# Putting the short contractions of two token mixers on all 128 rows of TensorE

## The chip, the cores and the metric

The kernel runs on one core of a Trainium2 chip. The metric is the device time of one execution in microseconds (us), and lower is better. A core has a matrix engine (TensorE, PE in the profile, with its weight loads listed apart as PEld), a vector engine (VectorE, DVE), a scalar engine (ScalarE, ACT), GpSimd (POOL) and SyncE (SP, here a DMA queue). A matmul contracts over the partitions (rows) of its two operands: the stationary one is loaded first, then the moving one streams past it. The profile writes the stationary operand as rows*columns and the moving one as rows x columns, so `16*128 16x256` is a contraction over 16 rows.

## The reference

A hybrid encoder of two layers works on 528 tokens (16 learned meta tokens and 512 others) with 1024 features. Each layer is a SwiGLU feed-forward half (hidden size 2816), a mixer, and a second feed-forward half. The change is in the mixer alone, which is cut here to what it touches:

```python
h = z @ w_in                       # one wide projection, split into the operands below
# branch A: gated linear attention, 4 heads, 64 key and 128 value features, forward and backward
gate = log_sigmoid(lr @ w2 + b2) / 16          # lr: 16 features for each direction (low rank)
b = cumsum(gate) inside a chunk
att = mask((q * exp(b)) @ (k * exp(-b)).T)     # scores inside a chunk, both directions
o_a = att @ v + (q * exp(b)) @ S               # S: state carried over the chunks
# branch B: softmax attention, 8 query heads on 2 key/value heads, 64 features each
p = softmax(rope(norm(q)) @ rope(norm(k)).T)
o_b = p @ v                                    # 528 keys: 4 blocks of 128 and 16 meta keys
y = sigmoid(g_a) * (o_a @ w_pa) + sigmoid(g_b) * (o_b @ w_pb)
out = y @ w_out
```

The last layer needs no output at the meta tokens, so most of its tensors are 512 wide, not 528.

## The kernel before

All activations are kept with features on partitions and tokens on the free axis. A product with a weight matrix runs in a split form: weight and operand each become a rounded part (`hi`, written by ACT) and a remainder (`lo`, written by DVE), both in the rounded matmul format fp32r, and three of the four partial products are accumulated. In the projections of the mixer that is three matmuls for each of eight 128-row slices and each half of the tokens (264 wide), 48 in all. In the narrow low-rank projection (32 columns) it is 48 as well. Weights come in slabs of 1024 columns over SP's queue, and `Weights.make` splits each of them up to four slabs ahead of its use.

Plain fp32 matmuls stand in the profile with two records each, fp32r matmuls and transposes with one.

The mixer (`mixer`) does in turn:

- four products for `r` and the low-rank product (into `lr`, 32 rows and a row of ones for the bias);
- twice (`gla_pair`, two heads each): projections of q, k and v; for each direction the decays, `z = w2t.T @ lr` on 33 rows; transposes of k and v to tokens on partitions; the end states of the blocks (`state(b)`, forward in rows 0 to 63 and backward in rows 64 to 127); the scores (64 rows: a head each in rows 0 to 63 and 64 to 127, two directions `d`) and the output, which adds `vtok @ scores` and `state(b) @ qin`. In the last block, NB - 1, only the forward state exists, so its product runs on 64 rows; for the meta block only the backward one does;
- `attention`: for two key/value heads, pairs of 128-query blocks. `probs` makes one block's scores and their softmax, `weighted` transposes the probabilities, splits them and multiplies by v. The 16 meta keys are a fifth part, the tail: a transpose to 16 partitions, a copy by ACT (`hi`), a subtraction by DVE (`lo`), and two matmuls on 16 rows. `weighted` runs 18 times in the first layer and 16 times in the second, so there are 34 tails;
- gates, merging, and the last product.

A scheduler orders the instructions of each engine, from the order in the code, the dependencies and its own costs. PE thus has projections of later steps (`project`, tiles `mm`) between the steps of the linear attention and of the softmax attention. Each engine then runs its list in that order.

Of the kernel before, what the change touches and what calls it, by code (L numbers as in the profile page):

```python
# [141 lines left out]
class Weights:  # L142
# [91 lines left out]
    def next(self, name):  # L234
        t = PLAN[self.pos]
        assert t[1] == name, (t, name)
        s, c = divmod(COLUMN[self.pos], SLAB)
        self.pos += 1
        hi, lo = self.use(self.at[s])
        return hi[:, c : c + t[5]], lo[:, c : c + t[5]]  # L240

    def op(self, *load):

# [5 lines left out]
def build(tc, ctx, xt, wts, win, par, w2, const, umask, out):  # L249
# [32 lines left out]
    def nm(p):  # L282
        count[0] += 1
        return f"{p}{count[0]}"
# [300 lines left out]
    def gla_pair(l, p, lr, w2t, sr, qa, ka, va, n_out):  # L585
# [17 lines left out]
        for d in range(2):  # L603
            z = pair()
            for i, hs in enumerate(halves):
                c0 = p * 256 + d * P
                TE.matmul(z[:, i, :HF], w2t[:33, c0 : c0 + P], lr[:33, hs], start=True, stop=True)
            a, g, c, ct_ = slot("t"), slot("t"), slot("t"), slot("t")

            S.activation(v2(a), z[:, :, :HF], AF.Abs)  # L610
            S.activation(a, a, AF.Exp, scale=-1.0)
            S.activation(a, a, AF.Ln, bias=1.0)
            V.scalar_tensor_tensor(v2(g), z[:, :, :HF], 0.0, v2(a), ALU.min, ALU.subtract)
            ones = ct[:, C_COS + SEQ : C_COS + SEQ + 1]
            for bs in [b[1] for b in blocks] + [MB]:
                n = bs.stop - bs.start
                V.tensor_tensor_scan(c[:, bs], ones.broadcast_to([P, n]), g[:, bs], 0.0, ALU.mult, ALU.add)
            mid = blk(c)[:, :, 63:64].broadcast_to([P, NB, P])
            tot = blk(c)[:, :, 127:128].broadcast_to([P, NB, P])
            mm_ = c[:, T - 1 : T].broadcast_to([P, META])  # L620
            r16 = 1.0 / 16.0
            src = c
            if d == 1:
                V.tensor_tensor(g, c, g, ALU.subtract)
                src = g

            def to_end():
                V.tensor_tensor(blk(ct_), blk(src), tot, ALU.subtract)
                V.tensor_tensor(ct_[:, MB], src[:, MB], mm_, ALU.subtract)


# [24 lines left out]
            if d == 0:  # L656
                S.activation(c, c, AF.Exp, scale=r16)
                ein, eq, ek = c, a, g
            else:
                S.activation(ct_, ct_, AF.Exp, scale=-r16)  # L660
                ein, eq, ek = ct_, g, a
            V.tensor_tensor(qp[:, :n_out], qa, eq[:, :n_out], ALU.mult)
            V.tensor_tensor(kp, ka, ek, ALU.mult)
            if qin is None:
                qin = [slot("p"), slot("p")]
            e0 = 127 if d == 0 else 0
            for hh in range(2):
                rows = slice(hh * HD, (hh + 1) * HD)
                to = slice(d * HD, (d + 1) * HD)
                V.tensor_tensor(qin[hh][to, :n_out], qa[rows], ein[rows, :n_out], ALU.mult)  # L670
                V.tensor_copy(dec[to, hh, :], blk(ein)[rows, :, e0])
            prods.append((qp, kp))
# [14 lines left out]
        def vtok(b, hh):  # L687
            return ktm[:META, 256 + hh * P : 256 + (hh + 1) * P] if b == NB else vk[hh][:, blocks[b][1]]

        for b in [NB, 0, 1, 2, 3]:  # L690
            ps = sm()
            for hh in range(2):
                TE.matmul(ps[:, hh * P : (hh + 1) * P], ktok(b, hh), vtok(b, hh), start=True, stop=True)  # L693
            pv = ps[:, :256].rearrange("p (h v) -> p h v", h=2)
            nxt = 0 if b == NB else b + 1
            if b == NB:
                S.copy(state(0)[0:HD], pv[0:HD])
            elif b < NB - 1:
                for hh in range(2):
                    V.scalar_tensor_tensor(state(nxt)[0:HD, hh], state(b)[0:HD, hh], dec[0:HD, hh, b : b + 1],  # L700
                                           pv[0:HD, hh], ALU.mult, ALU.add)
            if b != NB:
                prv = NB if b == 0 else b - 1
                S.copy(state(prv)[HD:P], pv[HD:P])
# [7 lines left out]
        for b in [3, 2, 1, 0] + [NB] * (n_out == T):  # L712
# [1 line left out]
            tt = slot("t")  # L714
            t3 = tt[:n, : 2 * n].rearrange("p (h i) -> p h i", h=2)
            ats = pair()
            for hh in range(2):
                rows = slice(hh * HD, (hh + 1) * HD)
                for d in range(2):
                    TE.matmul(ats[:n, hh, d * n : (d + 1) * n], prods[d][1][rows, bs], prods[d][0][rows, bs],  # L720
                              start=True, stop=True)

# [2 lines left out]
            op = sm()  # L725
            for hh in range(2):
                os_ = op[:, hh * n : (hh + 1) * n]
                rows = slice(0, P) if b < NB - 1 else (slice(0, HD) if b == NB - 1 else slice(HD, P))
                TE.matmul(os_, vtok(b, hh), t3[:, hh], start=True, stop=False)  # L729
                TE.matmul(os_, state(b)[rows, hh], qin[hh][rows, bs], start=False, stop=True)  # L730
            for hh in range(2):
# [22 lines left out]
    def attention(l, x, rs, n_out):  # L754
# [11 lines left out]
        vp, vpm = vpp[:, 0], vpp[:, 1]  # L766
        for c in range(NB):
            TE.transpose(vp[:, c * P : (c + 1) * P], vt[:, c * P : (c + 1) * P], ident)
        TE.transpose(vpm[:META, :P], vt[:, MB], ident)
        vs = []  # L770
        for g in range(2):
            rows = slice(g * HD, (g + 1) * HD)
            vv = slot("k", F32R)
            vm = small.tile([META, P], F32R, tag="vm", name=nm("vm"), bufs=2)
            v3 = vv[:, :512].rearrange("p (c f) -> p c f", c=NB)
            src = vp.rearrange("p (c f) -> p c f", c=NB)[:, :, rows]
            S.copy(v3[:, :, 0:HD], src)
            V.tensor_tensor(v3[:, :, HD:P], src, v3[:, :, 0:HD].bitcast(F32), ALU.subtract)
            S.copy(vm[:, 0:HD], vpm[:META, rows])
            V.tensor_tensor(vm[:, HD:P], vpm[:META, rows], vm[:, 0:HD].bitcast(F32), ALU.subtract)  # L780
            vs.append((v3, vm))

        bt = [None] * 4
# [47 lines left out]
        def group(g, ctx):  # L831
# [23 lines left out]
            def weighted(prs, n):  # L855
# [14 lines left out]
                o = sm()  # L870
                tp = o[:, 256:512]
                for u, pr in enumerate(prs):
                    TE.transpose(tp[:META, u * n : (u + 1) * n], pr[:n, MB], ident[:n, :n])
                tail = slot("lr", F32R)
                hi, lo = tail[:META, :256], tail[:META, 256:512]
                S.copy(hi[:, :w], tp[:META, :w])
                V.tensor_tensor(lo[:, :w], tp[:META, :w], hi[:, :w].bitcast(F32), ALU.subtract)
                parts.append((vs[g][1], hi[:, :w], lo[:, :w]))
                for i, (vw, ph, pl) in enumerate(parts):
                    TE.matmul(o[:, :w], vw, ph, start=i == 0, stop=False)  # L880
                    TE.matmul(o[:, :w], vw, pl, start=False, stop=i == len(parts) - 1)  # L881
                return o

            def both_rows(j, cs, o):
# [33 lines left out]
    def mixer(l, norm, done, following):  # L918
# [1 line left out]
        x, n_out = norm.x, T if l < DEPTH - 1 else SEQ  # L920
        pools = open_pools("left", e=8, i=5, p=7, q=6, k=5, lr=1)
        banks = open_pools("left", psum=("mm", "sm"), mm=2, sm=2)
        w2t = one.tile([33, 512], F32, tag="w2", name=nm("w2"))
        S.dma_start(w2t, w2[l])
        rp = [product("w_in", Acc(k, n_out), x, KC) for k in ("ss", "sm", "mm")]
        rs = norm.rs()
# [5 lines left out]
            sr.append(r)  # L932
        table("natural_log_exp_and_others")
        lr = slot("lr")
        ps = product("w_in", Acc("sm"), x, KC, width=32)
        scaled(lr, ps, rs, 1.0, slice(0, 32))
        V.memset(lr[32:33], 1.0)
        for p in range(2):
            qa = project(x, rs, "i", 0.125, n_out)
            ka = project(x, rs, "i")  # L940
# [153 lines left out]
```

## Time and profile before

| | |
|---|---|
| median of 3 runs | 2274.95 us (2274.92 to 2277.56) |
| the profiled execution: its own time | 2273.0 us |
| its span, first to last instruction | 2271.2 us |
| granted TensorE clock, mean | 0.992 |
| first mixer, about | 350 to 860 us of the span |
| second mixer, about | 1490 to 1960 us |

The profiled execution is 1.95 us below the median. Busy times of PE are modelled and overlap, since matmuls are pipelined: what a matmul costs in a full stream is the step from its start to the start of the next one, not its duration. In a timeline, consecutive instructions of one form are merged into one row, with the start of the first and their number.

### The profile page before, as it was taken

The page shows a single profiled execution, that of the slowest core. Times are in us where ns is not written, and L with a number is a line of the kernel's source. Part 1 is how long each engine was busy: PE and PEld are TensorE (multiplying, and loading weights), DVE is VectorE, ACT ScalarE, POOL GpSimd, SP SyncE. Part 2 cuts the span into 40 slices and gives each one's busy share as a digit, 9 for nine tenths or more (in the row PEclk, how much of TensorE's full clock was granted, in tenths as well). Part 3 has the DMA queues.
Part 4 walks back from the last instruction along what each step waited for, and adds up shares of the span by engine and source line. Part 5 has one row for each costly group of instructions (what it writes and reads, how often), then busy time and mean ns, then how long its engine had stood idle before and what let it go on. Part 6 is the DMA issues. An engine that isn't in the chain of part 4 may idle for free.

```text
span 2271.2 us, 39827 instructions
## 1 busy us (share of the span) xinstructions
PE 2219.0 (98%) x16548; PEld 2105.0 (93%) x16548; DVE 1512.6 (67%) x2387; ACT 1192.1 (52%) x1761; POOL 159.3 (7%) x186
## 2 busy tenths in 40 slices
PE   6999999999999999999989999999999999999997
PEld 5999999989999999999989999998788888989896
DVE  6657567476876676565676565674868667756566
ACT  7535355354785574453565353543457846636353
POOL 1111010000000010101001110100000001101010
PEclk9999999999999999999989999999999999999998
DMA  8868572212113485867657685632121136858661
GB/s 229 236 157 225 142 174 94 75 49 75 38 38 112 121 215 151 198 171 175 178 145 197 153 219 148 167 102 75 57 67 46 47 121 169 211 157 216 166 174 59
DMA packets 88412, 315.19 MB, mean 139 GB/s; under 512 B 9830, under 2 KB 12262, under 8 KB 88232
## 3 DMA queue, kind: packets, MB, share of 16 engines
q1 hardware_dynamic: 61136, 218.26, 28.9%
q0 software_dynamic: 25344, 92.29, 22.9%
q8 instruction: 130, 2.13, 0.4%
q10 hardware_dynamic: 1752, 2.11, 0.3%
q14 instruction: 50, 0.41, 0.1%
HBM read 264.38 MB, written 2.10 MB: 117 GB/s over the span
## 4 chain that ended last, share of the span: by engine, by line
PE 94%; DVE 3%; ACT 1%; DMA 1%; issue 0%; SPq 0%; DVEq 0%; POOL 0%; ACTq 0%
PE ss L497 39%; PE ss L377 27%; PE mm L377 15%; PE sm L377 3%; PE sm L863 1%; PE sm L880 1%; PE ss L838 1%; PE sm L881 1%; PE ss L383 1%; PE ss L839 1%; PE sm L693 1%; PE ss L720 0%; PE sm L729 0%; DVE wlo L222 0%; PE sm L730 0%
## 5 line engine op out<-in xcount | busy, mean ns | idle before, releaser
L497 PE MATMUL ss<-xc,whi 128*128 128x264 f32 (+1 forms) x4928 | 901.4, 285 | 25.4 <-ACT whi L221 9.2
L497 PEld LDWEIGHTS ss<-xc,whi 128*128 128x128 f32 x4928 | 766.2, 189 | 28.0 <-ACT whi L221 9.9
L497 PE MATMUL ss<-xc,wlo 128*128 128x264 f32 (+1 forms) x2464 | 701.7, 285 | 3.5 <-DVE wlo L222 3.5
L377 PE MATMUL ss<-g,whi 128*128 128x264 f32 (+2 forms) x2668 | 494.2, 301 | 0.0
L497 PEld LDWEIGHTS ss<-xc,wlo 128*128 128x128 f32 x2464 | 465.6, 189 | 4.5 <-DVE wlo L222 4.3
L377 PEld LDWEIGHTS ss<-g,whi 128*128 128x128 f32 x2668 | 388.6, 188 | 17.4
L377 PE MATMUL mm<-x,whi 128*128 128x264 f32 (+1 forms) x1712 | 384.0, 315 | 0.0
L221 ACT CAST whi<-w 128x1024 fp32r<-128x1024 f32 (+1 forms) x221 | 230.9, 1047 | 260.5 <-PE ss L377 118.0
L221 ACT CAST whi<-raw 128x1024 fp32r<-128x1024 f32 x190 | 199.3, 1049 | 299.7 <-PE mm L377 108.4
L222 DVE TENSOR_TENSOR wlo<-w,whi 128x1024 fp32r<-128x1024 f32 (+1 forms) x221 | 267.8, 1218 | 108.7 <-ACT whi L221 106.3
L377 PE MATMUL ss<-g,wlo 128*128 128x264 f32 (+2 forms) x1334 | 310.0, 301 | 0.0
L222 DVE TENSOR_TENSOR wlo<-raw,whi 128x1024 fp32r<-128x1024 f32 x190 | 232.1, 1221 | 106.8 <-ACT whi L221 105.6
L377 PEld LDWEIGHTS mm<-x,whi 128*128 128x128 f32 x1712 | 278.4, 188 | 18.8 <-issue 2.6
L377 PE MATMUL mm<-x,wlo 128*128 128x264 f32 (+1 forms) x856 | 266.1, 315 | 0.0
L377 PEld LDWEIGHTS ss<-g,wlo 128*128 128x128 f32 x1334 | 213.4, 188 | 8.7
L222 DVE TENSOR_TENSOR wlo<-s,whi 128x1024 fp32r<-128x1024 f32 x88 | 107.6, 1223 | 101.7 <-ACT whi L221 101.7
L221 ACT CAST whi<-s 128x1024 fp32r<-128x1024 f32 x88 | 92.4, 1051 | 153.3 <-PE ss L497 134.8
L377 PEld LDWEIGHTS mm<-x,wlo 128*128 128x128 f32 x856 | 159.6, 188 | 10.4 <-issue 2.1
L464 DVE SCALAR_TENSOR_TENSOR t<-ss,rs 128x528 f32<-128x528 f32 (+1 forms) x95 | 66.0, 700 | 127.3 <-PE ss L377 127.2
L172 ACT ACTIVATE s<-w 128x1024 f32<-128x1024 f32 x88 | 93.3, 1060 | 81.1 <-DMA w<-win 43.4
L177 POOL DMA_DIRECT2D w<-win x44 | 38.9, 883 | 973.7 <-DVE wlo L222 402.4
L503 ACT COPY snap<-ss 128x528 f32<-128x528 f32 (+1 forms) x132 | 77.1, 584 | 0.0
(232 smaller groups left out, 2597.5 us busy)
## 6 DMA issues: line engine op xcount, KB each, us to landing
w<-win SPq DMA_DIRECT2D x219, 512.0 KB, 4.6
raw<-wts SPq DMA_DIRECT2D x190, 512.0 KB, 3.4
s<-win POOLq DMA_DIRECT2D x44, 512.0 KB, 6.8
w<-s POOLq DMA_DIRECT2D x44, 512.0 KB, 5.6
w<-win POOLq DMA_DIRECT2D x44, 512.0 KB, 6.7
s<-w POOLq DMA_DIRECT2D x44, 512.0 KB, 7.2
h<-xt SPq DMA_DIRECT2D x3, 528.0 KB, 6.4
out<-h SPq DMA_DIRECT2D x4, 256.0 KB, 2.3
```

Source lines behind the costliest of these rows:

```text
L172: self.nc.scalar.activation(t, w, AF.Copy, scale=-1.0)
L177: self.nc.gpsimd.dma_start(t, src, accum_op=ALU.add)
L221: nc.scalar.copy(hi[:, cs], w[:, cs])
L222: nc.vector.tensor_tensor(lo[:, cs], w[:, cs], hi[:, cs].bitcast(F32), ALU.subtract)
L377: TE.matmul(acc.half[i][:width], lhs, rhs[:, acc.spans[i]], start=first, stop=last)
L383: TE.matmul(a, weights, x[:, hs], start=True, stop=True)
L464: V.scalar_tensor_tensor(cut(dst[rows]), pv[rows], -0.5 * f, cut(rs[rows]), ALU.mult, ALU.mult)
L497: TE.matmul(acc[:, j], a[:, j, k], b[:, at], start=bool(begin and k == 0 and i == 0), stop=k == len(x) - 1 and i == 2, skip_group_check=no ...
L503: S.copy(st[name], acc)
L693: TE.matmul(ps[:, hh * P : (hh + 1) * P], ktok(b, hh), vtok(b, hh), start=True, stop=True)
L838: TE.matmul(s[:n, i, :HF], lhs, kh[:, hs], start=True, stop=False)
L839: TE.matmul(s[:n, i, :HF], lhs, kl[:, hs], start=False, stop=True)
```

## The change

1. Tails: v of the meta tokens is written twice into a zeroed tile of 128 columns (`vz`), which is transposed into a value tile of 128 rows. The last 64 columns of the probabilities are transposed, not the last 16; ACT writes `hi` into rows 0 to 63 and DVE `lo` into rows 64 to 127 of one tile, and one matmul on 128 rows takes the place of two on 16.
2. Decays: `w2t` and `lr` are padded to 128 rows, with zero weights.
3. End states: rows 64 to 127 of the state of the last block are zeroed, and its product runs on 128 rows. The meta block's stays on 64 rows.
4. Scores: the loops over heads and directions change places, so that heads take turns.
5. Low-rank product: `hi` and `lo` of the narrow weights are copied side by side into one tile of 64 columns (by ACT and DVE), and each operand part is multiplied by both at once: 32 matmuls, not 48. It now forms all four partial products; the halves are added in the decays' product, whose weights are repeated.

```diff
+    def row(self, name, n):
+        first = self.next(name)
...
+        self.pos += n - 1
+        return [t[:, c : c + n * width] for t in self.got[self.at[s]]]
...
-                TE.matmul(z[:, i, :HF], w2t[:33, c0 : c0 + P], lr[:33, hs], start=True, stop=True)
+                TE.matmul(z[:, i, :HF], w2t[:, c0 : c0 + P], lr[:, hs], start=True, stop=True)
...
+        V.memset(state(NB - 1)[HD:P], 0.0)
...
-            for hh in range(2):
-                rows = slice(hh * HD, (hh + 1) * HD)
-                for d in range(2):
+            for d in range(2):
+                for hh in range(2):
+                    rows = slice(hh * HD, (hh + 1) * HD)
                     TE.matmul(ats[:n, hh, d * n : (d + 1) * n], prods[d][1][rows, bs], prods[d][0][rows, bs],
                               start=True, stop=True)
...
-                rows = slice(0, P) if b < NB - 1 else (slice(0, HD) if b == NB - 1 else slice(HD, P))
+                rows = slice(0, P) if b != NB else slice(HD, P)
...
-        TE.transpose(vpm[:META, :P], vt[:, MB], ident)
+        vz = slot("t")[:, :P]
+        V.memset(vz, 0.0)
+        for e in (HD, P):
+            V.tensor_copy(vz[:, e - META : e], vt[:, MB])
+        TE.transpose(vpm[:, :P], vz, ident)
...
-                    TE.transpose(tp[:META, u * n : (u + 1) * n], pr[:n, MB], ident[:n, :n])
-                tail = slot("lr", F32R)
-                hi, lo = tail[:META, :256], tail[:META, 256:512]
-                S.copy(hi[:, :w], tp[:META, :w])
-                V.tensor_tensor(lo[:, :w], tp[:META, :w], hi[:, :w].bitcast(F32), ALU.subtract)
-                parts.append((vs[g][1], hi[:, :w], lo[:, :w]))
+                    TE.transpose(tp[:HD, u * n : (u + 1) * n], pr[:n, T - HD :], ident[:n, :n])
+                tail = slot("lr", F32R)[:, :w]
+                S.copy(tail[:HD], tp[:HD, :w])
+                V.tensor_tensor(tail[HD:P], tp[:HD, :w], tail[:HD].bitcast(F32), ALU.subtract)
                 for i, (vw, ph, pl) in enumerate(parts):
                     TE.matmul(o[:, :w], vw, ph, start=i == 0, stop=False)
-                    TE.matmul(o[:, :w], vw, pl, start=False, stop=i == len(parts) - 1)
+                    TE.matmul(o[:, :w], vw, pl, start=False, stop=False)
+                TE.matmul(o[:, :w], vs[g][1], tail, start=False, stop=True)
...
-        ps = product("w_in", Acc("sm"), x, KC, width=32)
-        scaled(lr, ps, rs, 1.0, slice(0, 32))
-        V.memset(lr[32:33], 1.0)
+        V.memset(lr, 1.0)
+        ps, both = Acc("sm"), slot("p", F32R)[:, : KC * HD].rearrange("p (k s m) -> p k s m", k=KC, s=2)
+        for i, (copy, t) in enumerate(zip((S.copy, V.tensor_copy), W.row("w_in", KC))):
+            copy(both[:, :, i], t.bitcast(F32).rearrange("p (k m) -> p k m", k=KC))
+        for k, parts in enumerate(x):
+            for j, xp in enumerate(parts):
+                for a, cs in zip(ps.half, ps.spans):
+                    TE.matmul(a[:HD], both[:, k].rearrange("p s m -> p (s m)"), xp[:, cs],
+                              start=k == 0 and j == 0, stop=k == KC - 1 and j == 1)
+        scaled(lr, ps, rs, 1.0, slice(0, HD))
```

The change also moves instructions, since the scheduler orders the new program anew. Two places on PE follow, before and after.

At the end of the first `weighted` of the first layer stand, before, the last products with v of the 128-key blocks (`q` the split probabilities, `k` the values), the two matmuls of the tail (`lr` the tail, `vm` the meta values), and the transposes of the next probabilities (`t`):

```order
L880 MATMUL sm_6334<-q_6330,k_5954 128x256
L881 MATMUL sm_6334<-q_6331,k_5954 128x256
L880 MATMUL sm_6334<-lr_6337,vm_5955 128x256
L881 MATMUL sm_6334<-lr_6337,vm_5955 128x256
L863 MATMUL sm_6385<-const,t_6299 128x128
```

The same place after the change:

```order
L895 MATMUL sm_6327<-q_6323,k_5947 128x256
L896 MATMUL sm_6327<-q_6324,k_5947 128x256
L897 MATMUL sm_6327<-lr_6330,vm_5948 128x256
L387 MATMUL mm_7426<-x_4044,whi_6021 128x264
L879 MATMUL sm_6377<-const,t_6292 128x128
```

The tail is one matmul, and a projection's matmul (`mm`) has moved in behind it. Between the first and the last product with v of a layer's attention, 372 projection matmuls stood in the first layer and 190 in the second; now there are 397 and 208.

In the first `gla_pair` of the first layer PE has before, around the scores of two blocks (`ss`; `p` are the scaled keys and queries of a direction) and the end states (L693):

```order
L720 MATMUL ss_5018<-p_4908,p_4909 128x128
L693 MATMUL sm_4978<-q_4857,q_4855 128x128
L693 MATMUL sm_4978<-q_4858,q_4856 128x128
L720 MATMUL ss_5003<-p_4954,p_4955 128x128
L720 MATMUL ss_5003<-p_4908,p_4909 128x128
L720 MATMUL ss_5003<-p_4954,p_4955 128x128
L720 MATMUL ss_5018<-p_4954,p_4955 128x128
L720 MATMUL ss_5018<-p_4908,p_4909 128x128
L720 MATMUL ss_5018<-p_4954,p_4955 128x128
L377 MATMUL mm_5275<-x_4001,whi_4798 128x264
```

After the change that place reads:

```order
L731 MATMUL ss_5006<-p_4895,p_4896 128x128 x2
L704 MATMUL sm_4966<-q_4844,q_4842 128x128
L704 MATMUL sm_4966<-q_4845,q_4843 128x128
L731 MATMUL ss_4991<-p_4941,p_4942 128x128 x2
L731 MATMUL ss_5006<-p_4941,p_4942 128x128 x2
L387 MATMUL mm_5205<-x_4226,whi_4785 128x264
```

A stretch of scores now takes both heads of a direction together. In the four calls of `gla_pair` PE had 18 separate stretches of scores, of 1, 1, 6, 8 and (in the first layer, 16 wide) 4 matmuls each time; now there are 22, in the first call 2, 2, 4, 4, 4 and twice 2 narrow ones, in the second 2, 1, 1, 4, 2, 6 and 4 narrow ones, in each of the last two 2, 1, 5 and 8.

In all, PE's list goes from 16285 matmuls to 16219, DVE's from 2379 instructions to 2391, ACT's from 1707 to 1709.

More of the change, by code (lines that the diff above doesn't have):

```diff
@@ L240, in next @@
         return hi[:, c : c + t[5]], lo[:, c : c + t[5]]
+    def row(self, name, n):
+        first = self.next(name)
+        width = PLAN[self.pos - 1][5]
+        s, c = divmod(COLUMN[self.pos - 1], SLAB)
+        assert all(t[1] == name and t[5] == width for t in PLAN[self.pos : self.pos + n - 1])
+        assert COLUMN[self.pos + n - 2] == s * SLAB + c + (n - 1) * width and c + n * width <= SLAB
+        self.pos += n - 1
+        return [t[:, c : c + n * width] for t in self.got[self.at[s]]]
     def op(self, *load):
@@ L773, in attention @@
             vv = slot("k", F32R)
-            vm = small.tile([META, P], F32R, tag="vm", name=nm("vm"), bufs=2)
+            vm = small.tile([P, P], F32R, tag="vm", name=nm("vm"), bufs=2)
             v3 = vv[:, :512].rearrange("p (c f) -> p c f", c=NB)
@@ L778, in attention @@
             V.tensor_tensor(v3[:, :, HD:P], src, v3[:, :, 0:HD].bitcast(F32), ALU.subtract)
-            S.copy(vm[:, 0:HD], vpm[:META, rows])
-            V.tensor_tensor(vm[:, HD:P], vpm[:META, rows], vm[:, 0:HD].bitcast(F32), ALU.subtract)
+            S.copy(vm[:, 0:HD], vpm[:, rows])
+            V.tensor_tensor(vm[:, HD:P], vpm[:, rows], vm[:, 0:HD].bitcast(F32), ALU.subtract)
             vs.append((v3, vm))
@@ L922, in mixer @@
         banks = open_pools("left", psum=("mm", "sm"), mm=2, sm=2)
-        w2t = one.tile([33, 512], F32, tag="w2", name=nm("w2"))
+        w2t = one.tile([P, 512], F32, tag="w2", name=nm("w2"))
         S.dma_start(w2t, w2[l])
@@ L1076 @@
     par[:, G_FIN:] = a["final_norm"].reshape(-1, P).T
-    w2 = np.zeros((DEPTH, 33, 512), np.float32)
+    w2 = np.zeros((DEPTH, P, 512), np.float32)
     for p in range(2):
@@ L1080 @@
             cs = slice(p * 256 + d * P, p * 256 + (d + 1) * P)
-            w2[:, d * 16 : (d + 1) * 16, cs] = a["gla_w2"][:, d, :, p * P : (p + 1) * P]
-            w2[:, 32, cs] = a["gla_b2"][:, d, p * P : (p + 1) * P]
+            for r in (d * 16, 32 + d * 16):
+                w2[:, r : r + 16, cs] = a["gla_w2"][:, d, :, p * P : (p + 1) * P]
+            w2[:, HD, cs] = a["gla_b2"][:, d, p * P : (p + 1) * P]
     const, umask = constants()
```

## The prediction

> **What bounds the kernel now.** I read the page first: what is busy, and the chain that ended last.
>
> ```profile
> PE 2219.0 (98%) x16548; PEld 2105.0 (93%) x16548; DVE 1512.6 (67%) x2387; ACT 1192.1 (52%) x1761; POOL 159.3 (7%) x186
> PE 94%; DVE 3%; ACT 1%; DMA 1%; issue 0%; SPq 0%; DVEq 0%; POOL 0%; ACTq 0%
> ```
>
> PE carries 94% of the chain. An average over stages could hide a mixer that waits for others, so I cut out the four stretches that the change touches, linear attention and softmax attention of each layer (columns: stretch, length, busy time of PE, PEld, DVE, ACT, POOL with their instructions, granted clock, DMA share, GB/s):
>
> ```profile
> 436.00:520.00 84.00, 82.08 (x622) 73.37 (x621) 63.79 (x150) 40.38 (x86) 0.00 (x0) 1.00 0.16 52
> 570.00:690.00 120.00, 119.99 (x934) 112.44 (x933) 95.72 (x237) 95.30 (x212) 0.00 (x0) 1.00 0.13 41
> 1573.00:1652.00 79.00, 77.89 (x481) 63.60 (x480) 62.43 (x144) 38.88 (x79) 0.00 (x0) 1.00 0.16 54
> 1705.00:1812.00 107.00, 106.97 (x647) 87.86 (x646) 86.39 (x197) 85.69 (x172) 0.00 (x0) 1.00 0.13 40
> ```
>
> PE has no idle time in the softmax attention and 1 to 2 us in each linear one; DVE and ACT are busy for at most 81%. So a step that PE no longer takes shortens the kernel, as long as nobody else is late. PE's busy share does not say how well it is used: that shows in the steps between starts. The stream's normal step stands in the low-rank product (start, length of the row, number at the end):
>
> ```profile
> 406.36 0.65 PE L377 MATMUL sm<-x,whi 128*32 128x264 f32 x4
> 406.84 0.42 PE L377 MATMUL sm<-x,wlo 128*32 128x264 f32 x2
> ```
>
> Four starts in 0.48 us: 0.12 us each. Now the end of the first `weighted`, with the transposes of a unit in the stream ahead of it:
>
> ```profile
> 577.13 0.60 PE L863 MATMUL sm<-const,t 128*128 128x128 f32 x4
> 577.48 0.37 PE L377 MATMUL mm<-x,whi 128*128 128x264 f32 x1
> ...
> 579.01 0.28 PE L881 MATMUL sm<-q,k 128*128 128x256 f32 x1
> 579.23 0.38 PE L880 MATMUL sm<-lr,vm 16*128 16x256 f32 x1
> 579.45 0.27 PE L881 MATMUL sm<-lr,vm 16*128 16x256 f32 x1
> 579.65 0.66 PE L863 MATMUL sm<-const,t 128*128 128x128 f32 x4
> 580.07 0.37 PE L377 MATMUL mm<-x,whi 128*128 128x264 f32 x1
> ```
>
> From the last 128-row matmul to the first on 16 rows 0.22 us pass, 0.22 to the second, and 0.20 to the next one on 128 rows; four transposes then take 0.42 us, against 0.35 in the stream. Where a projection follows, the delay afterwards is plainer:
>
> ```profile
> 586.43 0.28 PE L881 MATMUL sm<-q,k 128*128 128x256 f32 x1
> 586.64 0.39 PE L880 MATMUL sm<-lr,vm 16*128 16x256 f32 x1
> 586.87 0.28 PE L881 MATMUL sm<-lr,vm 16*128 16x256 f32 x1
> 587.07 0.39 PE L377 MATMUL mm<-x,wlo 128*128 128x264 f32 x1
> 587.30 0.41 PE L377 MATMUL mm<-x,whi 128*128 128x264 f32 x2
> ```
>
> Four steps make 0.87 us where four of the stream make 0.48. PE is shown busy all the while. I read it so: a change of the number of rows in use costs about 0.1 us at each of two steps on entering and two on leaving.
>
> **Part 1, tails.** Afterwards there is one matmul on 128 rows, so 0.36 us (three steps) for 0.87 where a projection or scores follow: 0.51 saved. Where transposes follow, 579.01 to 580.07 is 1.06 us; afterwards it is 0.12 for the tail, 0.12 to the transposes and 0.35 for them, 0.59: 0.47 saved, and 0.12 less where the transposes have to wait for their own data and their weights cannot be loaded ahead. I take 0.40 for these. In the timeline 21 of the 34 tails are followed by transposes, 13 by others: 21 x 0.40 + 13 x 0.50 = 14.9 us. Ends: 0.35 and 0.51 for all, 11.9 and 17.3. The wider transposes (64 columns) and the value tile (128) load more columns at the same number of matmuls; the 32-column loads above keep the step of the 128-column ones, so I take nothing for them.
>
> **Part 2, decays.** Two plain fp32 matmuls are four records. On 33 rows, and on 128 rows at the mean of squares (L383, same shape otherwise):
>
> ```profile
> 436.96 1.16 PE L607 MATMUL ss<-lr,w 33*128 33x264 f32 x4
> 438.05 0.39 PE L377 MATMUL mm<-x,wlo 128*128 128x264 f32 x1
> ...
> 390.05 1.05 PE L383 MATMUL ss<-t,const 128*128 128x264 f32 x4
> 390.75 0.73 PE L377 MATMUL sm<-x,whi 128*128 128x264 f32 x3
> ```
>
> 1.09 us from their first start to the next form's, against 0.70: 0.39 saved for each of 8 (2 directions, 4 calls), 3.1 us. The ends: 0.29 where one step still waits, and 0.5 with the delay on entering: 2.3 and 4.0.
>
> **Part 3, end states.** The product with the last block's state, twice in each of four calls, amid its neighbours on 128 rows:
>
> ```profile
> 465.96 0.48 PE L730 MATMUL sm<-p,q 64*128 64x128 f32 x2
> 466.38 0.49 PE L729 MATMUL sm<-t,q 128*128 128x128 f32 x2
> 466.80 0.49 PE L730 MATMUL sm<-p,q 64*128 64x128 f32 x2
> 467.21 0.49 PE L729 MATMUL sm<-t,q 128*128 128x128 f32 x2
> 467.54 0.28 PE L730 MATMUL sm<-p,q 128*128 128x128 f32 x1
> ...
> 467.76 0.39 PE L729 MATMUL sm<-t,q 128*128 128x128 f32 x2
> 467.98 0.39 PE L730 MATMUL sm<-p,q 128*128 128x128 f32 x2
> 468.30 1.26 PE L720 MATMUL ss<-p,p 64*128 64x128 f32 x16
> 469.49 0.39 PE L377 MATMUL mm<-x,whi 128*128 128x264 f32 x1
> ```
>
> Eight records take 1.58 us (465.96 to 467.54). On 128 rows two take 0.22 (467.76 to 467.98), so eight take 0.88: 0.70 saved in each call, 2.8 us; with the first step on entering at most 3.1.
>
> **Part 4, scores.** They stay on 64 rows; what may change is the overlap of the heads and the number of stretches. The row at 468.30 has eight matmuls, 16 records, in 1.19 us; one after the other they would need 16 x 0.11 = 1.76. So the heads overlap already. And in the stretch of six, where the program has one head, then the other twice, then again:
>
> ```profile
> 461.98 1.16 PE L720 MATMUL ss<-p,p 64*128 64x128 f32 x12
> 463.07 0.51 PE L377 MATMUL mm<-x,whi 128*128 128x264 f32 x2
> ```
>
> 12 records in 1.09 us: the 8 records of the head that has four matmuls, at 0.11, and one delay of each kind. A head's records set the time. In the first call this makes 2 + 2 + 8 + 8 = 20 steps before, nearer 21 since 1.19 us at 468.30 is one step above the perfect eight; afterwards 2 + 2 + 4 + 4 + 4 = 16: 0.5 us less. But there is one more wide stretch, and a narrow one more, each with a delay of about 0.35 us (half of part 3's 0.70): 0.7 us more. In the second call it is a little worse, in the last two (as many stretches, 2 + 2 + 6 + 8 steps) 0.3 better. Over the four I take 0; ends 2 us either way.
>
> The Trainium skill, "TensorE: Matmul & The Clock Gate", Part 3, says that small contractions in different row groups run at the same time, but that matmuls start and end strictly in program order. By that, two of one head in a row would have blocked the other head, and taking turns would save some steps in each block. The rows at 461.98 and 468.30 show less time than that order allows, so I keep 0, and the rule's case is a rival.
>
> **Part 5, low rank.** 16 matmuls fewer in each layer, 32 x 0.12 = 3.9 us. The ends are the same, since PE was in an unbroken stream there. The copies into the joint tile stand on ACT and DVE right behind the slab's own split, ahead of the norm's chain, before the slab is due.
>
> **What is added elsewhere.** DVE has 12 instructions more (4 clears of a state, 2 of `vz` with 4 copies, 2 copies of low-rank weights), ACT two. The nearest row, 256 wide:
>
> ```profile
> 577.52 0.40 DVE L877 TENSOR_TENSOR lr<-sm,lr 16x256 fp32r<-16x256 f32 x1
> ```
>
> At 0.4 us each that is 4.8 us on DVE and 0.8 on ACT. PE's projections cover them (DVE is idle for 20 and 17 us of the linear stretches); uncovered, all of it is 5.6 us, which is the upper end, and nothing in it can gain, so the lower is 0. I take 0. The wider `w2t` is one DMA in each mixer, asked for at its start, long before its use.
>
> **Sum.** 14.9 + 3.1 + 2.8 + 0 + 3.9 = 24.7 us of PE's steps. Against the profiled execution that is 2273.0 - 24.7 = 2248.3; the median lies 1.95 above it, so 2250. The bounds together: a gain of at most 17.3 + 4.0 + 3.1 + 2 + 3.9 = 30.3 (2244.7), and at least 11.9 + 2.3 + 2.8 - 2 + 3.9 - 5.6 = 13.3 (2261.7).
>
> **Rivals.**
> - Taking turns pays more. If matmuls start in program order, a block's four (8 records) take 7 steps before and 4 after, 3 x 0.11 x 16 blocks = 5.3 us more: 2245. Against it stands part 4. That is the rule of the Trainium skill's page named in part 4. Chance 0.07.
> - The attention stops being bound by PE. At 80% DVE and ACT are near enough: a tail's 0.4 us of slack less in each unit may turn into a wait for the softmax. If two thirds of part 1 go that way, 10 us are lost: 2260. For it: PE has little slack in its order. Against it: the new order puts 25 and 18 more projection matmuls inside the attention, and projections are left over behind it. Chance 0.12.
> - The change does not do what it says: the 0.22 us steps come from waiting for the tail's data, not from the rows. Then the padded tail still takes its 0.22, decays and states keep theirs, and only the second matmul (34 x 0.22 = 7.5) and part 5 go: 2274.95 - 11.4 = 2263.5. Against it: DVE had finished the tail at 577.92, 1.3 us ahead of its use, and steps before and after a 64-row product look the same with no new data due. Chance 0.04.
> - Slower: the one tail matmul cannot begin with `hi` while `lo` is on its way; PE stands still until DVE has written it, with all that is queued behind. In the first unit DVE is done 1.2 us before the new use (577.92 against 579.13). It decides only when DVE slips by that and another (24.7 + 4.5) / 34 = 0.86 us in the mean of all tails: a slip of 2.4 us would give 34 x 1.2 - 24.7 = 16 us more, 2291. Nothing in the change makes DVE that late. Chance 0.04.
>
> **Numbers.** My forecast has a chance of 0.73. The range 2244 to 2261 takes in its bounds and the first two rivals and leaves out under 2 in 10. A difference of 0.2% (4.5 us) is about what a measurement of this kernel can tell from none. Faster by more has 0.95 (forecast and the first three rivals, less 0.01 where the second takes all), slower 0.03, within it 0.02 (small cases of the second and fourth).
>
> **What would show it.** Right: no step of 0.2 us around a tail, one `vm` matmul of 128 rows x34 that starts 0.12 us behind its forerunner; the decays' four records in 0.7 us; no 64-row L730 except at the meta block; 64 low-rank matmuls with 64 columns; the attention stretches some 7 us shorter each, with PE still without idle time. Wrong: waits of PE for ACT or DVE in the attention, steps of 0.22 us that stay at the tail, or more stretches of scores with idle time between. Idle time of PE ahead of the transposes of the scaled keys would mean that the linear attention is bound by its chain.

## Result, and the profile after

| | before | after |
|---|---|---|
| median of 4 runs | 2274.93 us (2273.71 to 2277.56) | 2258.43 us (2257.32 to 2259.99) |
| the profiled execution, its span | 2273.0, 2271.2 us | 2259.0, 2257.2 us |

The ratio is 0.9926 [0.9909, 0.9944]: 16.5 us faster, where 24.7 were forecast. The first part of the page and the shares of the chain, after:

```profile
PE 2202.5 (98%) x16482; PEld 2098.4 (93%) x16482; DVE 1517.0 (67%) x2399; ACT 1194.2 (53%) x1763; POOL 159.2 (7%) x186
PE 90%; DVE 6%; ACT 3%; DMA 1%; issue 1%; SPq 0%; DVEq 0%; POOL 0%; ACTq 0%
```

PE's share of the chain fell from 94% to 90%, those of DVE and ACT rose from 4% to 9% together. The mixed-row steps themselves did what was forecast. PE's timeline after, first a tail with transposes behind it, then the end states, the low-rank product and the decays (columns as in the prediction):

```profile
644.79 0.28 PE L896 MATMUL sm<-q,k 128*128 128x256 f32 x1
644.91 0.28 PE L897 MATMUL sm<-lr,vm 128*128 128x256 f32 x1
645.03 0.27 PE L879 MATMUL sm<-const,t 128*128 128x128 f32 x1
...
464.64 0.38 PE L740 MATMUL sm<-t,q 128*128 128x128 f32 x2
464.86 0.39 PE L741 MATMUL sm<-p,q 128*128 128x128 f32 x2
465.08 0.39 PE L740 MATMUL sm<-t,q 128*128 128x128 f32 x2
...
408.00 1.25 PE L959 MATMUL sm<-x,p 128*64 128x264 f32 x9
...
436.66 1.16 PE L617 MATMUL ss<-lr,w 128*128 128x264 f32 x4
437.46 0.48 PE L387 MATMUL mm<-x,wlo 128*128 128x264 f32 x1
437.77 0.40 PE L387 MATMUL mm<-x,whi 128*128 128x264 f32 x2
```

The tail takes one step of 0.12 us (L897), and the next begins 0.12 us behind it. The end states go on at 0.22 us for two records. The decays' four records (L617) take 0.80 us here, where 1.09 stood; of the eight such rows four take the priced 0.70, the others 0.77 to 0.80. What did not follow shows when each softmax attention is cut out, from its first scores to its last product with v, and the stretch from there to the next feed-forward half (columns as for the stretches in the prediction). Before, then after, the first layer's two rows ahead of the second's:

```profile
563.40:686.60 123.20, 122.91 (x958) 115.19 (x956) 100.08 (x247) 97.47 (x214) 0.00 (x0) 1.00 0.13 41
686.60:795.90 109.30, 109.30 (x896) 109.05 (x897) 71.49 (x117) 52.87 (x82) 4.40 (x5) 1.00 0.43 122
1692.85:1807.90 115.05, 114.95 (x695) 94.45 (x693) 94.38 (x217) 90.52 (x184) 0.00 (x0) 1.00 0.14 47
1807.90:1911.10 103.20, 103.20 (x445) 83.08 (x445) 69.27 (x103) 52.66 (x77) 4.40 (x5) 1.00 0.45 125
```

```profile
561.70:684.30 122.60, 121.53 (x964) 115.45 (x962) 101.51 (x246) 98.92 (x214) 0.00 (x0) 1.00 0.14 44
684.30:789.85 105.55, 105.55 (x872) 105.34 (x872) 71.51 (x117) 52.48 (x82) 4.40 (x5) 1.00 0.44 125
1683.50:1798.50 115.00, 114.54 (x696) 94.68 (x696) 97.91 (x219) 90.57 (x184) 0.00 (x0) 1.00 0.15 49
1798.50:1897.40 98.90, 98.90 (x428) 79.86 (x427) 67.52 (x101) 51.98 (x77) 4.39 (x5) 1.00 0.46 129
```

The attentions kept their length (0.60 and 0.05 us shorter). Their gain shows in the stretches behind them, which are 3.75 and 4.30 us shorter, since 25 and 18 projection matmuls moved forward. PE's shown idle time in the attentions rose from 0.39 to 1.53 us.

**The balance.** I added up, over all of PE's starts in a mixer (from the last matmul of one feed-forward half to the first of the next), by how much each step exceeds the stream's for its form (0.121 us at 256 or 264 columns, 0.218 at 512, 0.110 at up to 128, 0.222 for a plain fp32 record of 264). A step is "near" when a contraction on fewer than 128 rows is next to it; "late" is the rest of the excess, less what some steps stay under the stream's.

| us | first mixer | second mixer |
|---|---|---|
| length | 443.55 to 435.69 | 420.77 to 412.19 |
| stream's steps | 422.31 to 418.22 | 389.34 to 385.47 |
| excess near a short contraction | 12.71 to 4.14 | 9.94 to 1.37 |
| late elsewhere | 8.52 to 13.33 | 21.49 to 25.35 |
| of it in softmax attention | 2.88 to 6.92 | 6.32 to 8.74 |
| of it in linear attention | 3.40 to 4.66 | 3.99 to 5.88 |

Steps worth 8.0 us and mixed-row excess of 17.1 us went: 25.1, where 24.7 were priced. But late steps of 8.7 us came in, and 16.4 us are left. That this is so near the median's 16.5 is in part chance: the profiled span fell by 14.0, since all that lies outside the mixers took 2.4 us longer in the profiled execution after.

Where a late step shows its cause, a buffer was not free or a tile not ready. PE's timeline after, in three places of the first attention, with a row of DVE behind (in brackets PE's shown idle time and what ended it):

```profile
592.35 0.40 PE L387 MATMUL mm<-x,whi 128*128 128x264 f32 x2
592.97 0.39 PE L854 MATMUL ss<-k,p 128*128 128x264 f32 x1 [0.22 <-ACT t L370]
593.20 0.29 PE L855 MATMUL ss<-k,p 128*128 128x264 f32 x1
...
638.01 0.37 PE L387 MATMUL mm<-x,whi 128*128 128x264 f32 x1
638.48 0.39 PE L854 MATMUL ss<-k,p 128*128 128x264 f32 x1
638.71 0.28 PE L855 MATMUL ss<-k,p 128*128 128x264 f32 x1
...
647.33 0.37 PE L387 MATMUL mm<-x,whi 128*128 128x264 f32 x1
647.82 0.38 PE L889 MATMUL sm<-const,t 128*64 128x128 f32 x2
...
646.98 0.69 DVE L883 TENSOR_TENSOR q<-sm,q 128x512 fp32r<-128x512 f32 x1
```

L854 is the first matmul of a block's scores. Its PSUM bank comes free with ACT's Exp of an earlier block (L370). At 592.97 it is 0.38 us late, of which 0.22 is shown as idle until ACT's Exp, and the step behind it takes 0.23, not 0.12. The tail's transposes (L889) start 0.49 us after their forerunner, 0.15 behind the end of DVE's split (646.98 + 0.69), which frees a bank of the same kind; the trace names no releaser there. In the attentions, steps over 0.15 us late numbered 3 and 4 before (0.77 and 0.88 us); now they are 12 and 9 (3.39 and 2.06). Ten of these are at a block's first scores, six at the tail's transposes.

### The profile page after: what moved, and what is told of

It reads as the page before. It is cut to its first block, busy times and chain, and to the rows that moved or that the text cites. A ratio compares the mean times of both kernels' runs of the same rounds, so it can differ in the third digit from the quotient of the medians.

```text
span 2257.2 us, 39713 instructions
## 1 busy us (share of the span) xinstructions
PE 2202.5 (98%) x16482; PEld 2098.4 (93%) x16482; DVE 1517.0 (67%) x2399; ACT 1194.2 (53%) x1763; POOL 159.2 (7%) x186
## 4 chain that ended last, share of the span: by engine, by line
PE 90%; DVE 6%; ACT 3%; DMA 1%; issue 1%; SPq 0%; DVEq 0%; POOL 0%; ACTq 0%
PE ss L507 39%; PE ss L387 28%; PE mm L387 13%; PE sm L387 2%; PE sm L879 1%; DVE wlo L222 1%; PE ss L393 1%; PE ss L854 1%; ACT t L370 1%; PE sm L895 1%; PE ss L855 1%; PE sm L896 1%; PE sm L704 0%; DVE t L627 0%; PE ss L731 0%
## 5 line engine op out<-in xcount | busy, mean ns | idle before, releaser
L387 PEld LDWEIGHTS ss<-g,whi 128*128 128x128 f32 x2668 | 388.7, 188 | 17.1
```

Source lines behind the costliest of these rows:

```text
L387: TE.matmul(acc.half[i][:width], lhs, rhs[:, acc.spans[i]], start=first, stop=last)
```

## The experiments

Theory A at the start was the prediction's: the rows' delays are real, and what is missing went where DVE is too late in the attention. Its rivals are named in the expectations. Each run is compared with "before" measured beside it on the same chip. The first four are parts of the change alone, or without one.

**Part 1 alone** (the tails and `vz` of the change's diff, on the kernel before):

> The kernel before with part 1 alone (padded tails). Theory A (the steps around short contractions go as priced, but PE then catches up with VectorE and ScalarE in the softmax attention and part of it returns as waits): the steps alone are worth 14.9 us; the trace of the whole change has about 5 us more waiting in the attention than before, so about 10 us faster, 2265 us, with 0.12 us steps around the tail and steps of 0.2 to 0.5 us in front of scores and tail transposes. Theory B (part 1 was over-priced, no waits return): about 7 to 8 us faster, 2267 us, and no more late steps than before. Theory C (the steps come from waiting for the tail's data): a step of 0.22 us stays ahead of the tail.

2266.96 against 2276.53 us, 0.9952 [0.994, 0.9965]: 9.6 us gained of 14.9 (8.0 to 13.7 by the interval). The steps show where the rest is: near excess 1.62 and 0 us in the two attentions, as after the whole change, and late steps of 6.88 and 8.75, also as after it; linear attention as before. So the loss in the attention comes from part 1 itself.

**Parts 2 and 3 alone** (decays on 128 rows, zeroed rows of the last state):

> The kernel before with parts 2 and 3 alone (decays and the last end state on 128 rows). Its order has 23 stretches of scores where before has 18. Theory A: priced at 5.9 us; five more stretches at 0.3 to 0.4 us each and waits for the scaled keys take some 3 to 4 us back: 2 to 3 us faster, 2272.5 us. Theory B (over-priced, no waits return): the steps themselves are smaller than 0.39 and 0.35 us for each product, and the idle time ahead of the transposes of the scaled keys does not grow.

2274.31 against 2276.53, 0.9987 [0.9979, 0.9996]: 2.2 us of the 5.9 priced. From the first decays to the last output of each layer's linear attention, near excess fell from 10.3 to 6.3 us, by 4.0. The five more stretches of scores are what is missing: with the step into each, all stretches take 19.3 us, and 17.0 before. Late steps in linear attention are 4.31 and 5.77 us (before 3.40 and 3.99).

**Part 4 alone, and the change without it:**

```diff
-            for hh in range(2):
-                rows = slice(hh * HD, (hh + 1) * HD)
-                for d in range(2):
+            for d in range(2):
+                for hh in range(2):
+                    rows = slice(hh * HD, (hh + 1) * HD)
```

> The kernel before with part 4 alone (heads in turn in the scores). The order keeps 18 stretches, 2, 1, 5, 8 and 4 narrow ones in place of 1, 1, 6, 8 and 4. Theory A (heads overlapped already): within 1 us of before, 2275 us. Rival (matmuls start in program order, so taking turns saves three steps a block): 5.3 us faster, 2269.6 us.

> The changed kernel without part 4 (directions inside heads, as before). Its order has 23 stretches of scores where the changed kernel has 22. Theory A: within 1 us of the changed kernel, 2258 us. Rival (taking turns pays): 5 us slower than it, 2263.5 us.

Alone: 2275.34, 0.9994 [0.9985, 1.0003]. The rest without it: 2260.79, 0.993 [0.9917, 0.9942], against 0.9926 with it. In time part 4 can't be told from nothing: alone it gains 3.4 us at most by its interval, so the prediction's first rival (5.3 us) falls; the pair with and without it is too coarse to decide that by itself. The traces show more. The stretches of scores, with the step into each, take 17.0 us before and 15.3 with part 4 alone, 19.3 in the change without it and 16.7 with it, and the near excess of linear attention is 6.3 us in the change without it and 3.8 with it. One block (8 records) takes 0.65 us either way, without turns and with them, where the rival had three steps of difference. Two blocks in one stretch (16 records) take 1.10 us in the run with part 4 alone and 1.19 before (468.30 in the prediction). The rows below are from the change without part 4, from the change, and from part 4 alone:

```profile
467.30 0.72 PE L731 MATMUL ss<-p,p 64*128 64x128 f32 x8
467.95 0.51 PE L387 MATMUL mm<-x,whi 128*128 128x264 f32 x2
...
465.62 0.72 PE L731 MATMUL ss<-p,p 64*128 64x128 f32 x8
466.27 0.51 PE L387 MATMUL mm<-x,whi 128*128 128x264 f32 x2
...
471.21 1.16 PE L720 MATMUL ss<-p,p 64*128 64x128 f32 x16
472.31 0.39 PE L377 MATMUL mm<-x,wlo 128*128 128x264 f32 x1
```

**Is it VectorE?** The second block's division by the softmax's sum, 0.5 us on DVE in each of 32 blocks, was moved to GpSimd, or left out in the kernel before and after.

```diff
-                    V.tensor_scalar(pr[:n], pr[:n], sc[:n, 2:3], None, ALU.mult)
+                    G.tensor_scalar(pr[:n], pr[:n], sc[:n, 2:3], None, ALU.mult)
```

> The changed kernel with one piece of the softmax moved from VectorE to GpSimd: the division of the second block's probabilities by their sum (33 instructions of 0.5 us). Theory A (part of the gain returns as waits for VectorE in the softmax attention): with 16 us of work off VectorE the late steps get fewer, up to 4 us faster than the changed kernel, 2254 to 2258 us, if GpSimd's own duration (its 128x256 products took 0.9 us, so about 1.9 us here) does not make the transposes late; if it does, slower than the changed kernel by up to 5 us, with PE waiting for GpSimd. Theory B (no waits return, part 1 over-priced): no change, 2258.4 us.

> The kernel before without that division on VectorE (left out: the second block of each pair keeps its undivided probabilities). Theory A: before, PE hardly waits in the attention (late steps of 0.8 and 0.9 us in the two layers), so 0 to 2 us faster than before, 2273 to 2275 us. Theory B: no difference between this and the next run in what the removal gains.

> The changed kernel without that division on VectorE (left out: the second block of each pair keeps its undivided probabilities). Theory A: the 6 us that returned in the attention come mostly from VectorE being late, so 3 to 6 us faster than the changed kernel, 2253 to 2255 us, and at least 2 us more gain than the same removal brings before the change. Rival: the waits are for ScalarE or for the buffers themselves, or there are none: within 1.5 us of the changed kernel.

On GpSimd: 2267.55 us, 0.9961 [0.9947, 0.9975], 9 us slower than after. The line's group and PE's waits in that kernel (least, median and most ns; then total us, times, longest):

```profile
L868 POOL TENSOR_SCALAR t<-t,sc x32: 1597/1604/2109, 568.9 to 1790.0; 128x528 f32<-128x528 f32 x32
PE sm L879 <- POOL t L868: 4.4, 6, 1.1
```

It took 1.60 us there, 0.50 on DVE, and PE waited: that run tells more of GpSimd than of DVE. The other two add no work elsewhere. Without the division, before is at 2276.7, 1.0 [0.999, 1.0009], and after at 2260.35, 0.9929 [0.9916, 0.9941]: no gain in either. The first layer's attention and the stretch behind it, after without the division:

```profile
562.40:679.20 116.80, 115.25 (x913) 108.94 (x911) 93.83 (x229) 96.77 (x211) 0.00 (x0) 1.00 0.13 42
679.20:791.65 112.45, 112.45 (x925) 112.24 (x924) 73.32 (x119) 54.57 (x84) 4.40 (x5) 1.00 0.43 122
```

The attention got 5.8 us shorter, and the scheduler left more projections for later (367 inside it where 397 were), so the rest got 6.9 longer. Late steps stay at 7.15 and 8.56 us. So less work on DVE brings nothing here, and theory A's forecast falls. It is not shown that PE never waits for DVE: the order was planned anew, with 30 fewer projections inside, so the run does not hold DVE's load apart from the order, and where more projections were put in (below), PE's idle time ahead of the tail's transposes does end with DVE's split (L883, 1.3 us in 2 waits). No run takes work off ACT in the softmax attention, though ten of the 21 late steps stand at first scores, whose bank ACT frees.

**Is it the length of the chain?** In linear attention the logarithm of the decays was left out (`S.activation(a, a, AF.Ln, bias=1.0)`, ACT).

> The changed kernel without the Ln in the decays of the linear attention (left out: the logarithm in the log-sigmoid; eight ScalarE instructions of 0.6 us, each in the chain from the decays' product to the scaled keys). Theory A (at the transposes of the scaled keys PE waits for that chain, after the change about 2.4 us more than before): the waits there shrink from 6 us to 2 or 3, so 3 us faster than the changed kernel, 2255.5 us. Rival (the linear attention is bound by PE's steps): within 1 us of it.

2259.15 against 2276.39, 0.9921 [0.9908, 0.9934]: no gain. Again the order has fewer projections there (598 for 603 matmuls and 467 for 473 in PE's records, all from projections), with late steps of 5.9 and 5.0 us.

This made theory D: the scheduler fills the mixer with just so many projections that its own costs say PE never waits. The mixed-row delays, which those costs would not hold (a guess), were slack on top. Without them PE arrives before banks are free. If so, with more projections in a call of `weighted` the whole price of a tail must show.

**More projections in the calls.** The gate's projections were written between the calls, one ahead of each of the first twelve, in the kernel after and before.

```diff
+                more()
                 both_rows(j, slice(b * P, (b + 2) * P), weighted(prs, P)[:, :256])
...
-        gates += [project(x, None, "g", n=n_out) for _ in range(2 * KC - EARLY)]
+        while len(gates) < 2 * KC:
+            more()
```

> The changed kernel with the twelve gate projections written into the attention, one ahead of each of the first twelve calls of weighted, not behind it: the order then has 581 and 299 projection matmuls inside the attention (397 and 208 in the changed kernel). Theory D (the order, planned without the steps of mixed row counts, leaves PE no time to spare ahead of data; those steps had hidden that the data come a little later than planned): with more projections ahead of them the late steps in the attention shrink from 3.4 and 2.1 us to under 2 and 1, and 3 to 5 us of what came back are gained, 2254 us, less what the end of the attention loses for lack of projections. Rival E (the data are late because VectorE and ScalarE are near their limit): late steps as before, 2258 us or more.

> The kernel before with the gate projections written into the attention in the same way (587 and 298 inside it, 372 and 190 before). Theory D: the steps around the short tails had covered the lateness, so little is gained, within 2 us of before, 2274 to 2276 us, and clearly less than the same edit gains after the change. Rival E: as in the run above, no gain either.

After: 2266.89 against 2275.23, 0.9961 [0.9947, 0.9975]. Before: 2284.64, 1.0041 [1.0028, 1.0054], where a change of up to 2 us was expected: a miss. In total both lost, and the late steps in the attention after the change rose to 12.3 and 11.4 us, where theory D had them shrink. (From the first to the last product with v both orders hold 505 and 264 projection matmuls, against 397 and 208 after and 372 and 190 before; the expectations' 581 to 587 and 298 to 299 are not counted over that stretch.) But the same two calls of the first layer can be laid side by side, with 47 and 48 projection matmuls in each kernel; after, then before (stretches from one call's last product to the next one's):

```profile
654.90:663.93 9.03, 9.03 (x77) 8.87 (x75) 6.05 (x14) 5.76 (x13) 0.00 (x0) 1.00 0.19 61
663.93:673.11 9.18, 9.18 (x77) 9.01 (x76) 6.06 (x14) 5.77 (x13) 0.00 (x0) 1.00 0.18 59
```

```profile
664.30:673.80 9.50, 9.50 (x77) 9.06 (x76) 5.88 (x14) 5.76 (x12) 0.00 (x0) 1.00 0.17 56
673.80:683.40 9.60, 9.60 (x78) 9.15 (x77) 5.86 (x13) 5.76 (x12) 0.00 (x0) 1.00 0.17 56
```

The difference is 0.47 and 0.42 us. Over four such calls, of 37 to 48 projection matmuls, the excess is 0.18 to 0.22 us after and 0.50 to 0.53 before, a difference of 0.32 on average, and with the matmul that fell away (0.12) the tail is worth 0.44 us, inside the priced 0.40 to 0.50. These four are the clearest. Of all 17 calls in both layers with 20 or more projection matmuls and the same number (give or take one) in both kernels, eleven differ by 0.25 to 0.37 us, five by -0.12 to 0.15 and one by 1.90; the nine with fewer differ by -0.18 to 0.20. In the scheduler's own order the excess of a call differs by 0.10 only (20.68 us before over 34 calls, 17.26 after), so 0.22 of it arrives. The loss in total is plain too: later calls of the first layer had 33, 7 and 5 projection matmuls left, and their excess is 2.29, 2.09 and 1.97 us (before, with 33, 2 and 10: 2.44, 3.46 and 2.68). In time the change is worth 17.8 us with the projections inside and 16.5 without, so the full price shows in those calls and not in the kernel.

**Spread more evenly.** One ahead of three calls in four (shown against the run before); then, as a stream that yields after each matmul, in pieces of 36 matmuls (18 in the second layer) ahead of every call.

```diff
-                more()
+                if i % 4 != 3:
+                    more()
```

> The changed kernel with the gate projections written ahead of three in four calls of weighted, spread over all of the attention (561 and 271 inside it). Theory D: as the run with twelve in a row, 2254 us, with the last units covered as well and the uncovered quarter of the calls still late. Rival E: 2258 us.

```diff
+        def stream():
...
+        def more(n=36):
+            for _ in range(n if n_out == T else n // 2):
+                next(rest, None)
```

> The changed kernel with the remaining gate projections cut into pieces of 36 matmuls (18 in the last layer), one piece written ahead of each call of weighted: 554 and 261 projection matmuls inside the attention, 17 to 51 in each call of its first layer's second half. In the runs with whole projections a call with 35 or more of them lost 0.2 us to late steps, one with few 0.4 to 2 us. Theory D: the calls of the second half in the first layer lose 0.2 us each, the others as in the changed kernel, so 2 to 4 us faster than it, 2255 us. Rival E (VectorE and ScalarE set the lateness): no call gets better, 2258 us or more.

2258.69 against 2275.23, 0.9924 [0.9911, 0.9937], and 2259.18 against 2274.51, 0.9924 [0.991, 0.9937]: both as after, not the 2254 and 2255 that theory D expected. Late steps in the attention are 7.5 and 9.5 us in the first, 6.9 and 9.2 in the second (after: 6.9 and 8.7). In the second, the five calls with 34 to 40 projections have 0.17 to 0.23 us of excess where after has 0.34 to 0.45: these calls do as expected, and the total does not move: what is put into them is missing from others. The call behind them has 19 projection matmuls left and 1.0 us of excess. No version beats the changed kernel.

## Why the prediction was right, and short by 8 us

- **Part 1, right in size, lost in part.** Priced 14.9 us. Gone from PE's steps in the attention: 10.1 of near excess and 34 x 0.12 = 4.1 of matmuls, 14.2. Late steps took 6.5 back. Alone it brought 9.6, where these steps make 7.7; single executions differ by that much.
- **Parts 2 and 3.** Priced 5.9; alone they took 4.0 us of near excess away and brought 2.2 (interval of the ratio: 0.9 to 4.8 us). Two terms were too large. The decays' rows reach 0.70 in only four of eight, and the step behind each is some 0.09 us longer than before (at 437.46 it takes 0.31); with the steps ahead and behind, 2.6 us went of the 3.1 priced. And the new order cuts the scores into more stretches, which cost 2.3 us.
- **Part 4.** Put at 0, with 2 us either way. Its time cannot be told from 0, but by the steps it is worth 2.5 us of near excess beside the other parts. In the whole change 6.5 us of near excess went in linear attention, near the 5.9 priced, and 3.2 came back as late steps: parts 2 and 3 fell short by about what part 4 added, which is luck in the sum. The prediction weighed a rule of the Trainium skill there ("TensorE: Matmul & The Clock Gate", Part 3: matmuls start and end strictly in program order); by it the change of loops would have brought some 5 us, and the runs disagree (0.9994 [0.9985, 1.0003]).
- **Part 5.** 5.68 to 3.72 and 5.67 to 3.70 us from first to last start: 3.9 as priced.
- **The step that failed** is in the first part: "So a step that PE no longer takes shortens the kernel, as long as nobody else is late." PE without idle time was read as PE alone in charge. The sum has no term for PE arriving too early at what others free, and 8.7 us of 25 came back as late steps. The "Against it" of the second rival pointed the wrong way: more projections inside the attention did not cover them, and with "the attention stretches some 7 us shorter each" it was the clearest miss. That rival had the right place and nearly the size (6.5 of 14.9 lost, not 10), but its reason, DVE and ACT being near their limit, was not confirmed: taking 0.5 us a unit off DVE changed nothing, and ACT was not tried.
- **The rivals against the sign** did not come: no wait at the one tail matmul for `lo` appears among PE's ten longest waits. That the 0.22 us steps came from data and not from rows is refuted by the padded tail, which takes 0.12 where that rival kept 0.22.
- **Added work** on DVE and ACT was taken as free. No run holds it apart; the low-rank stage, where two of the copies stand, has its full gain.

Shown: the terms of the steps and their places, that part 1 alone brings its late steps with it, and that the full price of a tail arrives in most calls with 20 or more projections, though not in all. Argued only: that the delays had covered the lateness because the scheduler's costs lack them; the smaller numbers of projections in the two lighter kernels fit it, but three runs from which theory D expected 2254 or 2255 us came out at 2258.7 to 2266.9. Open: whether any order has cover enough for all calls, and how much of the lateness ACT sets. The releaser of most late steps is not in the trace either, since only a few show as idle time.

## What to carry to other kernels

An engine that shows no idle time may still have delays that hide its neighbours' lateness. When you take them away, price not only the steps but how far ahead of its data the engine then runs, at each buffer that another engine frees. Count late steps between starts, near and away from the change, and check that the second number stays. Here making a neighbour faster bought nothing, since the scheduler took filling out again; where a scheduler plans the gaps, compare its filling before and after as well as the times.

## What the runs showed of the hardware

- A change of the rows in use costs PE time on the way in and out: four steps around a tail take 0.87 us (586.43 to 587.30 before), the stream's 0.48, and 0.32 us of that came off in the four covered calls. The Trainium skill, "TensorEngine Tiling (Array Packing)", Key Properties, says that a switch of the array's mode needs a drain; the trace has a delay where the rows change and gives it this price, but does not show that a drain takes it. Fewer columns cost nothing: the low-rank product with 64 keeps 0.12 us a step (nine in the row at 408.00, 31 steps in 3.72 us).
- A late first matmul of a block's scores is late twice: behind all ten of these the next step took 0.22 to 0.23 us (592.97 and 638.48 among them), while behind those that came on time behind a projection or a tail it took 0.12 to 0.23 (0.12 in eight of them). It is not so everywhere: behind the six late transposes of the tail it took 0.11 to 0.13.
- One block's scores, four matmuls on 64 rows, take 0.65 us whether or not the two row halves alternate in the program (467.30 in the change without part 4, 465.62 with it).
- On GpSimd an elementwise product of 128x528 took 3.2 times as long as on VectorE (1.60 and 0.50 us).
